# One projection for the context of all groups, and softmax division on the outputs, in the second attention of a two-layer trunk

## The chip, the cores and the metric

The kernel runs on one core of a Trainium2 chip. The metric is the time of one execution on the device, in microseconds (us). The five engines that the text names are TensorE (PE, with PEld for its weight loads), VectorE (DVE), ScalarE (ACT), GpSimd (POOL) and SyncE (SP), whose queue issues the DMA transfers. Each engine works through its own list of instructions in order and waits for the others by semaphores.

## The reference

A trunk of two layers over 1024 latent tokens and 256 context tokens, width 1024, 16 heads of 64. Layer 0 mixes by neighbourhood attention, layer 1 by sliding-window attention with grouped keys: four groups, each with four query heads, one key head and one value head. Every layer ends with a gated feed-forward network that has a convolution in it. In layer 1 the context has keys and values only, since its own stream ends there.

```
def attn_inputs(h, w_qkv, g_q, g_k, n_kv, with_q=True):
    ...
        kv = h @ w_qkv[:, D_MODEL:]
    k = rmsnorm(kv[..., :kv_w].reshape(bsz, t, n_kv, HEAD_DIM), g_k)
    v = kv[..., kv_w:].reshape(bsz, t, n_kv, HEAD_DIM)
...
def attend(q, k, v, bias=None, mask=None, sink=None):
    s = einsum(q, k) * HEAD_DIM ** -0.5      # and mask
    if sink is not None:
        s = concatenate([s, sink_col], axis=-1)
    p = softmax(s, axis=-1)[..., :-1]        # without the sink's column
    return einsum(p, v)
...
    # layer 1: queries see |i - j| <= 128 and all 256 context keys
    x = x + gt1 * (o @ w_out)
    h = modulate(rmsnorm(x, g_ffn[i]), sh2, sc2)
    x = x + gt2 * conv_ffn(h, ...)
```

All is float32. The kernel gets that accuracy from a fast product of rounded operands by splitting each operand into a rounded part (hi) and a remainder (lo) and adding three products: hi by hi, lo by hi, hi by lo.

## The kernel before

The kernel is a chain of stages: the first attention, the feed-forward of layer 0 (`ffn`, line 1246), the second attention (lines 2098 to 2350), the feed-forward of layer 1. Inside a stage the order of work is not written by hand. Each operation is given to a planner (`Sched`, line 61) with an engine (or a choice of two), a supposed duration, what it reads and writes, the ring buffers that it takes and gives back, and a rank (`key`). The planner plays a list schedule at build time, lower rank first among what is ready, and the instructions are issued in the order that comes out, one fixed order for each engine. So a change of a duration, a ring or a rank moves the whole stage, and an instruction that the chip finds late holds up everything behind it on its engine.

The rings that matter here are counted in `CAPS` (line 945): three raw buffers of 128x1024 for whatever a DMA brings in, four pairs of split weights (`w`, hi and lo), five probability rows `S`, two accumulators `mm`, two transposed blocks `pt`, two outputs `osb`. A ring gives out its buffers in turn, so the oldest has to be free before the next is taken.

The second attention has these kinds of operations.

- `plan_sw_qkv` (line 2118) makes queries, keys and values of one tile of 128 tokens for one group. Ten tiles belong to a group, in the order of `ORDER` (line 327): the two context tiles 8 and 9 first, then the latent tiles 0 to 7. A latent tile is 24 products of 384 columns (four query heads, a key head, a value head); a context tile is 24 products of 128 columns, since only key and value are wanted. Then come the norm over each head (a power on POOL, three small steps on DVE), rotation, the split into hi and lo, transposes on PE and copies to the key and query buffers. The ranks run from 16g, 1.6 for each tile.
- The weights of a group are four slabs (`Slabs`, line 405), each loaded into a raw buffer and split by ACT and POOL. The four slabs of group 0 are loaded and split in the feed-forward before (`plan_next`, line 2089, `AHEAD`), and stay in the four weight pairs over the stage's boundary.
- `plan_sw_su` (line 2245) with `plan_su` (line 504) is the attention of one block of 128 queries for one pair of heads, 16 of them in a group, ranks 16g + i + 7.5 (`LEAD1`). Scores against 256 context keys and up to 384 latent keys; on DVE the negated scores with mask and running minimum; on ACT the exponential with its sum (`exp`, line 563); on DVE the reciprocal of the sum (`rec`); on DVE or ACT the scaling of the 512 or 640 probabilities by it (`scale`, line 573). Then five transposes for each of the two heads, split, and products with the values, hi and lo packed side by side; the two halves are added into `osb`.
- For groups 0 to 2 the outputs go to memory (`o_dram`) and are fetched again at the end, since the buffers that hold the normed input are in use until the last QKV product. The last group's outputs stay on the chip.
- `plan_oproj1` (line 2315) is the output projection of the first 512 tokens: 8 blocks of 128 output columns, 24 products of 512 columns each, with rank 1000 (`OKEY`) and more, that is, after everything else. The fetched outputs are split into buffers that alias the normed input, so this may not start before the last QKV product of group 3 (`op1.gate`); the loads of outputs have the same gate, the loads of the projection's weights one a few tiles earlier (`w_gate`). The second 512 tokens are projected at the beginning of the feed-forward that follows.

Of the kernel before, what the change touches and what calls it, by code (L numbers as in the profile page):

```python
# [17 lines left out]
P = 128  # L18
# [208 lines left out]
def trunk_kernel(ctx, tc, xperm, xseq, cc, wmod, bmod, gnorm, na_wqkv, na_gq, na_gk, na_bias, na_wo,  # L227
                 sw_wqkv, sw_gq, sw_gk, sw_sink, sw_wo, rope_c, rope_s, band, w_up, conv, w_down, out):
# [15 lines left out]
    c_dram = dpool.tile([P, KT * TC], F32, name="c_dram")  # L244
    xa_dram = dpool.tile([P, KT * T], F32, name="xa_dram")
# [258 lines left out]
    def plan_su(sc, key, I, units, groups, psa, wk, reads, write, n_add):  # L504
# [28 lines left out]
        for k in range(2):  # L533
# [435 lines left out]
    AHEAD, NPRE = 4, 3  # L969
# [118 lines left out]
    def plan_na_su(n):  # L1088
# [71 lines left out]
        plan_su(sc, key, I, units, groups, psa, wk, reads, write, 1)  # L1160
# [859 lines left out]
    def plan_next(sc, KS, xn, bank, x_tile, plan_sums, plan_bc, plan_t, plan_hilo, u_done):  # L2020
# [68 lines left out]
        for i in range(AHEAD):  # L2089
            key = KS[5] - 4  # L2090
            sc.op("dma", 1.4, lambda e, i=i: slabs.load(i), reads=[("dw", 4, FT // 2 - 4, "r")], writes=[("slr", i)], key=key,
                  acq=[("raw", ("slr", i), 2)])
            sc.op("act", t_act(768), lambda e, i=i: slabs.hi(i), reads=[("slr", i), ("dw", 4, FT // 2 - 1, "wl", 0)],
                  writes=[("slh", i)], key=key, acq=[("w", ("slw", i), 1)], rel=[("slr", i)])
            sc.op("dve", 0.87, lambda e, i=i: slabs.lo(i, e), reads=[("slr", i), ("slh", i)],
                  writes=[("sll", i)], key=key, rel=[("slr", i)])

    slabs = Slabs(sw_wqkv, WL1)
    slabs.n_ahead = AHEAD
# [15 lines left out]
    op1 = Oproj(sc, 1, 0, 512, psa, [("q1", NKV - 1, tt, "acc") for tt in range(NT)], [],  # L2115
                [("q1", NKV - 1, WG1, "acc")])

    def plan_sw_qkv(n):
        g, tt = n // NT, ORDER[n % NT]
        key = n / NT * 16 + QKEY1  # L2120
        lat = tt < 8
# [3 lines left out]
        nh, c0 = (5, 0) if lat else (1, 256)  # L2125
        f = F1.setdefault(g, dict(q=[None] * 8, v=[None] * NT))
# [10 lines left out]
        def vhi(e):  # L2137
            vt = f["v"][tt] = fin.tile([P, P], F32R, tag="v" if lat else "vc", name="v", bufs=8 if lat else 4)
            copy(e, vt[:, 0:DH], J["raw"][:, 320:384])
        vuses = 2 * ((tt > 0) + 1 + (tt < 7)) if lat else 16  # L2140
        sc.op("act", t_act(64), vhi, reads=[K("raw")], writes=[K("vh")], key=key,
              acq=[("v" if lat else "vc", vk, vuses)], rel=[K("raw")])
# [7 lines left out]
        def qn(e):  # L2150
            J["qn"] = wk.tile([P, 5, DH], F32, tag="qn", name="qn", bufs=2)
            ENG[e].tensor_tensor(out=J["qn"][:, 5 - nh:], in0=J["raw"][:, c0:320].rearrange("p (h d) -> p h d", d=DH),
                                 in1=J["y"][:, :nh].unsqueeze(2).to_broadcast([P, nh, DH]), op=ALU.mult)
        sc.op("dve", t_dve(nh * DH), qn, reads=[K("raw"), K("y")], writes=[K("qn")], key=key,
              acq=[("qn", K("qn"), 2 if lat else 1)], rel=[K("raw")])
        spans = ((0, slice(0, 4), 4), (1, slice(4, 5), 1))
        if lat:
            def qa(e):
                J["a"] = wk.tile([P, 5, DH], F32, tag="qa", name="qa", bufs=2)
                for k, s, m in spans:  # L2160
                    ENG[e].tensor_tensor(out=J["a"][:, s], in0=J["qn"][:, s], in1=rc[:, tt, k:k + 1, :].to_broadcast([P, m, DH]),
                                         op=ALU.mult)
            sc.op(*QA, qa, reads=[K("qn")], writes=[K("a")], key=key, acq=[("qa", K("a"), 4)], rel=[K("qn")])

            def qb(e):
                J["b"] = wk.tile([P, 5, DH], F32, tag="qb", name="qb", bufs=2)
                for k, s, m in spans:
                    for d0, d1 in ((0, 32), (32, 0)):
                        ENG[e].tensor_tensor(out=J["b"][:, s, d0:d0 + 32], in0=J["qn"][:, s, d1:d1 + 32],
                                             in1=rs[:, tt, k:k + 1, d0:d0 + 32].to_broadcast([P, m, 32]), op=ALU.mult)  # L2170
            sc.op(*QB, qb, reads=[K("qn")], writes=[K("b")], key=key, acq=[("qb", K("b"), 1)], rel=[K("qn")])

            def qs(e):
                ENG[e].tensor_tensor(out=J["a"], in0=J["a"], in1=J["b"], op=ALU.add)
            sc.op("pool", t_pool(320), qs, reads=[K("b")], writes=[K("a")], key=key, rel=[K("b")])
        else:
            def qa(e):
                J["a"] = wk.tile([P, 5, DH], F32, tag="qa", name="qa", bufs=2)
                ENG[e].tensor_tensor(out=J["a"][:, 4], in0=J["qn"][:, 4], in1=gqk[:, 1, :], op=ALU.mult)
            sc.op(("pool", "dve"), (t_pool(64), t_dve(64)), qa, reads=[K("qn")], writes=[K("a")], key=key,  # L2180
                  acq=[("qa", K("a"), 2)], rel=[K("qn")])
# [13 lines left out]
        if lat:  # L2195
            def qhi(e):
                J["qhi"], J["qlo"] = [J["st"][:, 0:4, x * DH:(x + 1) * DH] for x in (0, 1)]
                act.activation(J["qhi"], J["a"][:, 0:4], AF.Copy)
            sc.op("act", t_act(256), qhi, reads=[K("a"), K("kd")], writes=[K("qh")], key=key, rel=[K("a")])

            def qlo(e):
                ENG[e].tensor_tensor(out=J["qlo"], in0=J["a"][:, 0:4], in1=J["qhi"].bitcast(F32), op=ALU.subtract)
            sc.op("pool", t_pool(256), qlo, reads=[K("a"), K("qh")], writes=[K("ql")], key=key,
                  rel=[K("a")])

        def trk(e):
# [4 lines left out]
              rel=[K("klt"), K("st")] + ([] if lat else [K("st")]))  # L2211
        kk, kl = (("kk", tt), ("kl", tt)) if lat else (("kkc", g), ("klc", g))
        first = [] if lat or tt == ORDER[0] else [kk, kl]

        def kev(e):
            if tt == ORDER[0]:
                f["kkc"] = fin.tile([P, TC], F32R, tag="kkc", name="kkc", bufs=2)
            dst = kkl1[:, tt * P:(tt + 1) * P] if lat else f["kkc"][:, (tt - 8) * P:(tt - 7) * P]
            copy(e, dst, J["pt2"][:, 0:P].bitcast(F32))
        sc.op("act", t_actp(128), kev, reads=[K("pt2")] + first, writes=[kk], key=key,  # L2220
              acq=[("kkc", kk, 32)] if tt == ORDER[0] else (), rel=[K("pt2")])

        def lev(e):
            if tt == ORDER[0]:
                f["klc"] = fin.tile([P, TC], F32R, tag="klc", name="klc", bufs=2)
            dst = kll1[:, tt * P:(tt + 1) * P] if lat else f["klc"][:, (tt - 8) * P:(tt - 7) * P]
            copy(e, dst, J["pt2"][:, P:2 * P].bitcast(F32))
        sc.op("act", t_actp(128), lev, reads=[K("pt2")] + first, writes=[kl], key=key,
              acq=[("klc", kl, 32)] if tt == ORDER[0] else (), rel=[K("pt2")])
        if lat:  # L2230
            def trq(e):
                J["pt"] = psa("pt", F32R)
                for i in range(4):
                    pe.transpose(J["pt"][:, i * P:(i + 1) * P], J["st"][:, i, :], idr)
            sc.op("pe", 0.43, trq, reads=[K("qh"), K("ql")], writes=[K("pt")], key=key, acq=[("pt", K("pt"), 1)],
                  rel=[K("st")])

            def qev(e):
                q = f["q"][tt] = fin.tile([P, 4, P], F32R, tag="q", name="q", bufs=8)
                copy(e, q.rearrange("p a b -> p (a b)"), J["pt"].bitcast(F32))  # L2240
            sc.op("act", t_actp(512), qev, reads=[K("pt")], writes=[qk], key=key, acq=[("q", qk, 8)], rel=[K("pt")])

    O = {}

    def plan_sw_su(n):
# [8 lines left out]
        for k in range(2):  # L2254
            hd = 2 * pr + k

            def get(hd=hd):
                q = f["q"][j]
                return dict(q=q[:, hd, :], kk=kkl1[:, ks], kl=kll1[:, ks], kkc=f["kkc"], klc=f["klc"],
                            mask=bandt[:, (lo - j + 1) * P:(hi - j + 2) * P], sink=sink[:, 4 * g + hd:4 * g + hd + 1])  # L2260
            units.append(dict(nl=(hi - lo + 1) * P, sink=1, get=get, mask_key=[], rel_c=[("q", g, j), ("kkc", g), ("klc", g)],
                              rel_l=[("q", g, j)]))
        reads = [("q", g, j), ("kkc", g), ("klc", g)]
        reads += [(x, t) for t in range(lo, hi + 1) for x in ("kk", "kl")]
        lst = [(8, 0), (9, P)] + [(b, TC + (b - lo) * P) for b in range(lo, hi + 1)]
        lst = [(lambda t=t: f["v"][t], ("v", g, t), [(0, c), (1, c)]) for t, c in lst]
        nj = 2 if g < NKV - 1 else 4
        ok = ("osb", g, j // nj, pr)
        heads = lambda t: t[0:DH].rearrange("p (h t) -> p h t", h=2)

        def write(sc, J, K):
            def add(e):
                if j % nj == 0:
                    f["o", pr] = O[j // 4, pr] = wk.tile([P, 512], F32, tag="osb", name="osb", bufs=2)
# [191 lines left out]
```

## Time and profile before

| what | value |
|---|---|
| median of 3 runs | 2849.25 us (2848.09 to 2849.77) |
| profiled execution | 2851.74 us |
| its span, first to last instruction | 2850.0 us |
| mean granted TensorE clock | 0.989 |
| PE busy over the span | 2784.4 us (98%) |
| DVE busy | 2324.1 us (82%) |
| ACT busy | 1713.2 us (60%) |
| POOL busy | 400.1 us (14%) |
| last product of the feed-forward before the stage | starts at 1677.55 us |
| first product of the next feed-forward stage | starts at 2145.18 us |

A row of windows gives a stretch in us from the start of the span, its length, then for each engine the busy time and in brackets the number of instructions, then the TensorE clock that was granted (1.00 is full), the share of the DMA engines in use, and GB/s. A row of the timeline gives start, duration, engine, line, operation, output and input tiles and, in square brackets, idle time before it and who ended it. A row of a group gives its form, how many there were, busy time and mean duration in ns, and idle time before them. All lines carry L51, a helper through which every instruction is recorded, so the tile names tell the operations apart: `mm` is an accumulator of QKV or of the projection, `h1chi` and `h1clo` the normed context, `S` the scores and probabilities, `sm` their sums, `slab` a raw weight slab, `oraw` a fetched output, `woraw` a raw block of projection weights. Matmuls are pipelined: a product's duration overlaps with that of the next, so dense products are counted by the distance of their starts.

### The profile page before, as it was taken

Reading aid. Unit: us, or ns where it says so; the run is one execution under the profiler, and the core shown is the slowest. Engines: PE = TensorE matmul, PEld = TensorE weight load, DVE = VectorE, ACT = ScalarE, POOL = GpSimd, SP = SyncE. Lnnn points to the kernel's source line nnn. Section 1 sums busy time; section 2 is a strip of 40 time slices with the busy share of each in tenths; the row PEclk is TensorE's granted clock in tenths of the full one; section 3 lists DMA queues with packets and bytes.
Section 4 is the critical chain, followed back from the end, with each engine's and each line's share of the span. In section 5 each row is a group of like instructions: output and inputs, shape, how many; then the busy total and the mean of one; then the engine's idle time right before and its main releaser. Section 6 shows DMA issues by size and latency. Waiting matters only on the chain.

```text
span 2850.0 us, 46124 instructions
## 1 busy us (share of the span) xinstructions
PE 2784.4 (98%) x16344; PEld 2455.3 (86%) x16344; DVE 2324.1 (82%) x5243; ACT 1713.2 (60%) x3382; POOL 400.1 (14%) x675
## 2 busy tenths in 40 slices
PE   6999999999999999999999999999999999999999
PEld 5999999998789987777788888999987788888887
DVE  7888888888688687877797787999987988888757
ACT  5877777778456554444454457888873554455443
POOL 1222212223000000000010006455520000000000
PEclk9999999999999999999999999999999999999999
DMA  6222222314745544444375551010234323324745
GB/s 247 65 95 80 83 67 75 96 60 125 250 142 192 183 162 140 154 142 160 135 258 194 181 169 29 13 34 16 73 128 138 116 105 111 111 93 149 253 148 182
DMA packets 140953, 367.20 MB, mean 129 GB/s; under 512 B 21425, under 2 KB 34225, under 8 KB 139313
## 3 DMA queue, kind: packets, MB, share of 16 engines
q1 hardware_dynamic: 140720, 364.25, 38.1%
q8 instruction: 129, 2.11, 0.3%
q14 instruction: 104, 0.84, 0.1%
HBM read 297.21 MB, written 66.98 MB: 128 GB/s over the span
## 4 chain that ended last, share of the span: by engine, by line
PE 69%; DVE 4%; ACT 2%; issue 1%; DMA 1%; DVEq 0%; ACTq 0%; SPq 0%
PE ua L51 17%; PE dn L51 15%; PE uc L51 13%; PE mm L51 6%; PE oacc L51 4%; PE ud L51 4%; PE pt L51 3%; PE pv L51 2%; PE dnc L51 2%; PE s L51 2%; DVE S L51 1%; PE mod L51 1%; ACT S L51 1%; DVE ptlo L51 1%; DVE x L51 0%
## 5 line engine op out<-in xcount | busy, mean ns | idle before, releaser
L51 ACT ACTIVATE whi<-wraw 128x512 fp32r<-128x512 f32 (+1 forms) x264 | 212.6, 806 | 203.6 <-PE uc L51 62.7
L51 DVE TENSOR_TENSOR wlo<-wraw,whi 128x512 fp32r<-128x512 f32 (+1 forms) x264 | 239.2, 907 | 45.3 <-ACT whi L51 44.8
L51 DVE TENSOR_TENSOR ptlo<-pt,pthi 128x512 fp32r<-128x512 f32 (+2 forms) x384 | 223.2, 595 | 48.6 <-ACT pthi L51 45.0
L51 PE MATMUL dn<-ghi,wlo 128*128 128x512 f32 x616 | 242.4, 394 | 0.0
L51 PE MATMUL dn<-ghi,whi 128*128 128x512 f32 x616 | 242.4, 394 | 0.0
L51 PE MATMUL dn<-glo,whi 128*128 128x512 f32 x616 | 242.3, 393 | 0.0
L51 ACT ACTIVATE pthi<-pt 128x512 fp32r<-128x512 f32 (+2 forms) x384 | 195.1, 524 | 71.1 <-PE pt L51 61.1
L51 ACT ACTIVATE S<-S,m 128x640 f32<-128x640 f32 (+3 forms) x288 | 220.8, 768 | 22.7 <-DVE m L51 19.6
L51 DVE SCALAR_TENSOR_TENSOR u<-c,cv,u 128x1023 f32<-128x1023 f32 x176 | 223.2, 1279 | 6.8 <-ACT u L51 5.8
L51 ACT ACTIVATE whi<-s 128x1024 fp32r<-128x1024 f32 (+1 forms) x120 | 113.3, 945 | 191.4 <-PE uc L51 137.4
L51 ACT ACTIVATE ghi<-graw 128x512 fp32r<-128x512 f32 x154 | 96.4, 631 | 190.2 <-PE dn L51 108.4
L51 PE MATMUL pt<-idr,S 128*128 128x128 f32 x1280 | 199.2, 278 | 6.8 <-DVE sm L51 2.6
L51 PE MATMUL mm<-whi,h0hi 128*128 128x384 f32 x512 | 181.1, 354 | 0.4 <-ACT qraw L51 0.4
L51 DVE TENSOR_TENSOR glo<-graw,ghi 128x512 fp32r<-128x512 f32 x154 | 105.4, 688 | 83.8 <-ACT ghi L51 76.4
L51 PE MATMUL mm<-wlo,h0hi 128*128 128x384 f32 x512 | 172.3, 337 | 0.0
L51 PEld LDWEIGHTS pt<-idr,S 128*128 128x128 f32 x1280 | 153.5, 143 | 17.4 <-DVE ptlo L51 3.9
L51 DVE TENSOR_TENSOR wlo<-s,whi 128x1024 fp32r<-128x1024 f32 (+1 forms) x120 | 129.6, 1080 | 40.6 <-ACT whi L51 40.5
L51 POOL TENSOR_TENSOR qy<-qv,mhalf 128x4 f32<-128x4 f32 (+2 forms) x120 | 126.2, 1052 | 227.0 <-DVE qv L51 197.0
L51 PE MATMUL pv<-ptlo,v 128*128 128x256 f32 (+1 forms) x688 | 153.9, 297 | 1.2 <-DVE ptlo L51 1.2
L51 PE MATMUL pv<-pthi,v 128*128 128x256 f32 (+1 forms) x688 | 147.7, 287 | 4.1 <-DVE osb L51 3.0
L51 PE MATMUL ua<-t12hi,whi 128*128 128x512 f32 x352 | 138.7, 394 | 5.5 <-ACT t12hi L51 3.9
L51 POOL TENSOR_TENSOR n1y<-n1v,mhalf 128x4 f32<-128x4 f32 (+1 forms) x9 | 9.2, 1025 | 953.3 <-DVE n1v L51 950.7
(315 smaller groups left out, 8906.4 us busy)
## 6 DMA issues: line engine op xcount, KB each, us to landing
wraw<-in_w_up_dram SPq DMA_DIRECT2D x132, 512.0 KB, 3.4
wm<-in_wmod_dram SPq DMA_DIRECT2D x80, 512.0 KB, 4.0
wraw<-in_w_down_dram SPq DMA_DIRECT2D x44, 512.0 KB, 3.5
graw<-g_dram SPq DMA_DIRECT2D x44, 512.0 KB, 4.4
wraw<-in_w_down_dram SPq DMA_DIRECT2D x88, 256.0 KB, 3.0
graw<-g_dram SPq DMA_DIRECT2D x66, 256.0 KB, 2.8
slab<-in_na_wqkv_dram SPq DMA_DIRECT2D x32, 384.0 KB, 3.7
woraw<-in_na_wo_dram SPq DMA_DIRECT2D x24, 512.0 KB, 4.4
```

The lines of the kernel that those rows point to most:

```text
L51: r = f(*a, **k)
```

## The change

Context keys and values are no longer made group by group. One step, `plan_ctx_kv`, projects both context tiles onto the 512 columns of all groups' keys and values (48 products of 512 columns), norms, splits and transposes them, and keeps them for the whole stage. The feed-forward before brings these weights (`sw_ckv`, four pieces of 128x1024) over the boundary instead of the four slabs of group 0, which are now loaded and split within the stage. The QKV step has eight tiles in a group, with ranks 2 apart.

The reciprocal and the scaling of the probabilities go. The sum of each exponential row is written to a column of a table (`RS`), and the unscaled probabilities are transposed and multiplied with the values. For each group (for the last one, each half) one reciprocal of the table, a transpose, a copy and a store put the reciprocals into memory (`r_dram`). They are fetched again, each row repeated over 64 partitions, beside the stored outputs, and the outputs are multiplied by them before they are split.

At the end of the plan the stored outputs of the first 512 tokens get ranks from 57 on instead of 994 on, the first two of them with the earlier gate `w_gate`, the first four weight blocks of the projection ranks from 60.5 instead of 1000. The second half of x for the residual goes to the buffer of the context keys and so waits for the last score products. The last outputs of group 3 use the ring `st`.

```
@@ plan_su
-               scale=-1.0, accum_out=J["sm"][:, k, 0:1])
+               scale=-1.0, accum_out=sums(k) if sums else J["sm"][:, k, 0:1])
             sc.op("act", t_act(n) + 0.187, exp, reads=parts, writes=[K("P", k)], key=key)
+            if sums:
+                continue
@@ plan_next
-        for i in range(AHEAD):
-            key = KS[5] - 4
-            sc.op("dma", 1.4, lambda e, i=i: slabs.load(i), ...)
+        for i in range(4):
+            key = KS[5] - 30
...
+            sc.op("dma", 1.8, load, ..., key=KS[5] - 4, acq=[("raw", ("slr", i), 2)])
+            sc.op("act", t_act(1024), hi, ..., key=key, acq=[("w", ("slw", i), 1)], rel=[("slr", i)])
+            sc.op("dve", t_dve(1024) + 0.03, lo, ..., key=key, rel=[("slr", i)])
@@
+    def plan_ctx_kv():
+        hh, hl = h[2]
+        for i in range(4):
+            def mm(e, i=i):
+                for tt in range(2):
...
+                    for k in (2 * i, 2 * i + 1):
+                        wh, wl = [a[:, k % 2 * 512:k % 2 * 512 + 512] for a in CW[i]]
+                        for m, (a, w) in enumerate(((hh, wh), (hl, wh), (hh, wl))):
+                            pe.matmul(acc[tt], a[:, k, sl], w, start=(k == 0 and m == 0), stop=(k == KT - 1 and m == 2))
+            sc.op("pe", 12 * t_pe(512), mm, writes=[("ckv", "acc")], key=-300, ...)
...
+            CK["k"] = hpool.tile([P, 8, 256], F32R, tag="hclo", name="ckc", bufs=1)
...
+                CK["v", tt] = fin.tile([P, NKV, P], F32R, tag="vc", name="vc", bufs=2)
@@ plan_sw_qkv
-        g, tt = n // NT, ORDER[n % NT]
-        key = n / NT * 16 + QKEY1
+        g, tt = divmod(n, 8)
+        key = n * 2 + QKEY1
@@
+    def plan_recip(g, js, key):
+        a, n = 4 * js[0], 4 * len(js)
+        def rec(e):
+            dve.reciprocal(RS[g][:, a:a + n], RS[g][:, a:a + n])
...
+            pe.transpose(RS["pt", g, a][:n, :P], RS[g][:, a:a + n], idf)
...
+            RS["sb", g, a] = fin.tile([32, P], F32, tag="rst", name="rst", bufs=2)
+            act.activation(RS["sb", g, a][:n], RS["pt", g, a][:n, :P], AF.Copy)
...
+        sc.op("dma", 0.6, lambda e: dma.dma_start(r_dram[g, a:a + n], RS["sb", g, a][:n]), ...)
+
+    def r_rows(kt, c, k):
+        a = 16 * c + 4 * (2 * (kt % 2) + k)
+        return r_dram[kt // 2, a:a + 4, :].rearrange("j q -> (j q)").unsqueeze(0).to_broadcast([DH, 512])
@@ plan_sw_su
+        ring = "osb" if g < NKV - 1 or j < 4 else "st"
...
+        if g < NKV - 1:
+            if i == 15:
+                plan_recip(g, list(range(8)), 16 * g + 17 + LEAD1)
+        elif i in (7, 15):
+            c = j // 4
+            plan_recip(g, list(range(4 * c, 4 * c + 4)), key)
...
+            sc.op("dma", 1.8, load, reads=[("rs", g, c)], writes=[rk], key=key, acq=[("raw", rk, 2)])
+            for p in range(2):
...
+                op1.split(c, (c, 2 * g + p), 512, ...)
@@ the plan of the stage
+    for i in range(4):
+        sc.hold("w", ("cw", i), 1)
+    plan_ctx_kv()
...
+        slabs.engs = WL1 if g else WL0
         for j in range(4):
-            if 4 * g + j >= slabs.n_ahead:
-                slabs.plan(sc, 4 * g + j, 16 * g + QKEY1 if g else -200, NT)
-        for k in range(NT):
-            plan_sw_qkv(NT * g + k)
+            slabs.plan(sc, 4 * g + j, 16 * g + QKEY1 if g else -200, 8)
+        for k in range(8):
+            plan_sw_qkv(8 * g + k)
@@ plan_oproj1
                     dma.dma_start(R[c, kt][:, :512], o_dram[1][kt, :, 512 * c:512 * c + 512])
+                    for k in range(2):
+                        dma.dma_start(R[c, kt][k * DH:(k + 1) * DH, 512:], r_rows(kt, c, k))
-                key = OKEY + 6 * (c - 1) + kt
-                sc.op("dma", 1.0, load, reads=[("od", kt, c)] + op1.gate, writes=[r], key=key, ...)
+                key = OKEY + kt if c else 57 + 0.5 * kt
+                gate = op1.gate if c or kt > 1 else op1.w_gate
+                sc.op("dma", 1.8, load, reads=[("od", kt, c), ("rs", kt // 2, c)] + gate, writes=[r], key=key - 0.5, ...)
+                sc.op(("pool", "dve"), ..., R[c, kt][:, :512] * R[c, kt][:, 512:] ..., key=key)
-            op1.weights(dt, sw_wo[dt % KT], OKEY + dt, KT, ...)
+            op1.weights(dt, sw_wo[dt % KT], 60.5 + dt if dt < 4 else OKEY + dt, KT, ...)
```

More of the change, by code (lines that the diff above doesn't have):

```diff
@@ L2230, in plan_sw_qkv @@
[L2230 to L2241, printed above, removed]
@@ L2273, in add @@
                 if j % nj == 0:
-                    f["o", pr] = O[j // 4, pr] = wk.tile([P, 512], F32, tag="osb", name="osb", bufs=2)
+                    f["o", pr] = O[j // 4, pr] = wk.tile([P, 512], F32, tag=ring, name="osb", bufs=2)
                 if g < NKV - 1:
@@ L2320, in load @@
                 dma.dma_start(xt[k].rearrange("p k t -> p (k t)"), x_dram[:, 2048 * k:2048 * (k + 1)])
-            sc.op("dma", 3.2, load, reads=op1.gate, writes=[("xc", k)], key=OKEY + k)
+            sc.op("dma", 3.2, load, reads=op1.gate + [("su1", NKV - 1, j, pr, "sc") for j in range(8) for pr in range(2)] * k,
+                  writes=[("xc", k)], key=OKEY + k)
         def evac(dt, I):
```

272 lines of the change are left out of this document (191 added, 81 removed).

## The prediction

> **What bounds the kernel now.** I looked at the page first, for the shares over the whole span, then at windows over the second attention (the only stretch the change touches), then at the timeline of TensorE (PE) and of the DMA queue at its two ends, last at the groups by form.
>
> ```profile
> span 2850.0 us, 46124 instructions
> ```
> ```profile
> core 0: us, PE busy (x) PEld busy (x) DVE busy (x) ACT busy (x) POOL busy (x), PEclk, DMA share, GB/s
> 1742.00:2057.00 315.00, 310.15 (x2295) 301.95 (x2294) 295.87 (x1048) 276.66 (x695) 168.79 (x349) 0.99 0.10 28
> 2057.00:2077.00 20.00, 16.22 (x83) 12.97 (x83) 18.82 (x62) 14.94 (x34) 14.40 (x21) 0.74 0.53 185
> 2077.00:2145.00 68.00, 68.00 (x396) 59.66 (x395) 54.86 (x141) 46.07 (x93) 12.19 (x21) 1.00 0.45 148
> 1678.00:1742.00 64.00, 58.84 (x336) 57.32 (x337) 46.69 (x141) 35.70 (x87) 25.39 (x46) 0.87 0.21 72
> ```
>
> The stage runs from 1678 to 2145. In its long middle (first row) PE is busy 310.15 of 315 us at clock 0.99, while VectorE (DVE) has 295.87 and ScalarE (ACT) 276.66. DVE is close, but PE is the full one. Only the two ends have holes: 64 us with 58.84 busy at clock 0.87, and 20 us with 16.22 busy at 0.74. So two things are worth time here: products that disappear, and holes at the ends. Relief of DVE or ACT in the middle is not.
>
> Busy times overlap from one product to the next, so the price of a product is its distance to the next one in a dense run. Three pairs of timeline rows give it: 384 columns, 128 columns (context rows of a middle group), 512 columns (the last feed-forward products).
>
> ```profile
> 1698.16 0.33 PE L51 MATMUL mm<-whi,h1hi 128*128 128x384 f32 x1
> ...
> 1698.68 0.33 PE L51 MATMUL mm<-whi,h1hi 128*128 128x384 f32 x1
> ```
> ```profile
> 1871.65 0.27 PE L51 MATMUL mm<-whi,h1chi 128*128 128x128 f32 x1
> ...
> 1872.32 0.28 PE L51 MATMUL mm<-whi,h1chi 128*128 128x128 f32 x1
> ```
> ```profile
> 1675.69 0.39 PE L51 MATMUL dn<-ghi,whi 128*128 128x512 f32 x1
> ...
> 1677.55 0.40 PE L51 MATMUL dn<-ghi,wlo 128*128 128x512 f32 x1
> ```
>
> Three steps in 0.52 us: 0.173 at 384 columns. Six in 0.67: 0.112 at 128. Eight in 1.86: 0.23 at 512. Four times the columns cost only twice the time; that is the core of the first part of the change.
>
> The holes, in windows cut where the granted clock changes (same columns):
>
> ```profile
> 1677.50:1680.90 3.40, 2.11 (x15) 1.56 (x15) 3.40 (x5) 2.31 (x4) 0.00 (x0) 1.00 1.01 383
> 1680.90:1684.30 3.40, 3.40 (x18) 3.39 (x17) 3.16 (x6) 1.43 (x4) 0.00 (x0) 0.50 0.96 289
> ...
> 1687.70:1691.10 3.40, 3.40 (x13) 3.40 (x13) 1.92 (x11) 0.94 (x4) 1.16 (x2) 0.50 0.77 298
> ...
> 1708.20:1711.60 3.40, 1.29 (x8) 0.97 (x7) 2.90 (x10) 1.37 (x4) 1.79 (x3) 1.00 0.00 0
> 1711.60:1715.00 3.40, 3.40 (x13) 3.40 (x12) 2.24 (x11) 1.18 (x4) 3.30 (x7) 0.50 0.02 5
> ...
> 1749.10:1752.60 3.50, 1.56 (x13) 1.27 (x11) 3.43 (x13) 3.45 (x8) 1.78 (x3) 1.00 0.35 112
> 1752.60:1756.00 3.40, 3.40 (x17) 3.21 (x17) 3.36 (x12) 2.57 (x10) 2.51 (x3) 0.50 0.17 41
> ...
> 2063.20:2066.60 3.40, 2.19 (x10) 1.43 (x11) 3.40 (x14) 1.94 (x5) 3.40 (x8) 1.00 0.84 311
> 2066.60:2070.00 3.40, 2.48 (x8) 1.33 (x7) 3.21 (x14) 3.40 (x10) 2.65 (x2) 0.50 0.14 48
> ```
>
> A window in which PE stood for 1.2 to 2.1 us is followed by one at clock 0.50, so a hole costs itself and up to 1.7 us more. After the hole at 1677.5 the clock stays at 0.50 for three windows (1680.9 to 1691.1).
>
> **The change part by part.**
>
> *Context products.* Before, each of four groups runs 48 products of 128 columns (8 slices, 3 terms, 2 context tiles); after, 48 products of 512 columns run once. In groups 1 to 3 the products vanish from the full PE: 3 x 48 x 0.112 = **-16.1 us**. Group 0 belongs to the start.
>
> *The start.* Two more edits meet here: the four weight pairs held over from the feed-forward now carry the context columns, so the slabs of group 0 have to be fetched and split inside this stage; and the second half of the norm runs beside it.
>
> ```profile
> 1710.83 0.45 PE L51 MATMUL mm<-whi,h1hi 128*128 128x384 f32 x1 [2.11 <-ACT qraw L51]
> ```
> ```profile
> 1682.79 67.45 SPq L51 DMA_DIRECT2D slab<-in_sw_wqkv_dram  x6
> ```
> ```profile
> slab<-in_sw_wqkv_dram SPq DMA_DIRECT2D x10, 384.0 KB, 3.5
> ```
> ```profile
> L51 ACT ACTIVATE whi<-slab 128x768 fp32r<-128x768 f32 x5 | 4.2, 843 | 2.0 <-PE dn L51 1.8 <-DMA slab<-in_sw_wqkv_dram 0.2
> ...
> L51 DVE TENSOR_TENSOR wlo<-slab,whi 128x768 fp32r<-128x768 f32 x4 | 3.6, 954 | 0.3 <-ACT whi L51 0.3
> ```
>
> Before, 33 us lie between the last feed-forward product (ends near 1677.8) and tile 4 (1710.83, after a wait of 2.11 for the norm). After: context products 48 x 0.23 = 11.0, to 1688.8. The queue is free for slabs at 1682.79 as before, behind the writing and reloading of x; the DMA engines are full (share 0.96, then 0.77 of 3.4 us) to about 1690.3. The wider splits ahead of the x evictions on DVE (0.954 x 1024/768 = 1.27 each, an estimate) move this by about one split: slab 0 lands near 1691.5, plus 0.84, 0.95 and two hand-overs: PE starts tile 0 near 1693.6, a hole of 4. Slabs 2 and 3 wait for a raw buffer (the norm's sums, then slab 0) and come 3.5 + 0.84 + 0.95 later, near 1699; until then the first halves of tiles 0 and 1 keep PE busy. Then four tiles of 24 x 0.173 = 16.6, one window at half clock as after the holes at 1708 and 1749 (1.7), and 24 small products (broadcast of the norm, transposes of the context keys) at 0.112 = 2.7: tile 4 near 1715, 4 later than before. But the norm started 3 us earlier and should be done, so no wait stands ahead of tile 4, and the half window behind it, at 1711.6, is gone (1.7): **+2 us**. Ends: -4 if the slabs land under the context products (no hole, no half window), +9 if slabs 2 and 3 are also waited for, one landing of 3.5 each. I take the middle because the queue's order is the same as before. The two accumulators wait for ACT to copy them before tiles 0 and 1 can start; the hole covers that, and without it it would cost two copies.
>
> Here a rule bears. The Trainium skill, "TensorE: Matmul & The Clock Gate", section "What's actually happening", lets the clock fall after at least one idle window of about 3.4 us and rise after one busy window. This trace disagrees on both: 1.3 us of standing sufficed at 1677.5, and three windows stayed at 0.50 with PE busy 3.40 of 3.40. By the rule my hole of 4 us costs one half window, the 1.7 I took; by the row at 1680.9 it may cost three, and the sum would be 3.4 us higher.
>
> *The division.* Per unit a reciprocal and a scaling of the probabilities go (128 of each).
>
> ```profile
> L51 DVE TENSOR_SCALAR S<-S,sm 128x640 f32<-128x640 f32 x60 | 36.0, 600 | 0.5
> ...
> L51 DVE RECIPROCAL sm<-sm 128x1 f32<-128x1 f32 x122 | 18.6, 155 | 4.4 <-ACT S L51 3.3
> ```
> ```profile
> L51 ACT ACTIVATE S<-S,sm 128x640 f32<-128x640 f32 x34 | 28.1, 829 | 4.6 <-DVE sm L51 4.4
> ```
> ```profile
> L51 DVE TENSOR_TENSOR ptlo<-pt,pthi 128x512 fp32r<-128x512 f32 x126 | 84.6, 683 | 4.6 <-ACT pthi L51 3.5
> ```
>
> That frees 36.0 + 18.6 us of DVE and 28.1 of ACT in these rows alone. In the middle it buys nothing, PE being full. It shortens the way from exponential to transpose, which counts where PE waits: the hole at 1749.1 (1.94 us, and 1.7 at half clock) lies under busy ACT and DVE; the one near 1728 I leave. I take **-3**, ends 0 and -7 (both holes). Added: five transposes of row sums of 128 columns at 0.112, **+0.6** on PE; five evictions, five stores of the sums, 32 broadcast loads, 16 multiplies of 128x512 at about 0.68 (the last row's size on DVE). Stores of groups 0 to 2 stand on the queue ahead of next-group slabs; those are asked for seven ranks early, so 0, and a landing of 3.5 if that cover goes. The wider splits at the end of the feed-forward lie under PE products: 0 beyond the shift counted above.
>
> *The end.* QKV products end near 2057; then PE has only attention until the output projection can begin, at 2076.53.
>
> ```profile
> 2076.53 0.61 PE L51 MATMUL mm<-o0hi,whi 128*128 128x512 f32 x1
> ```
> ```profile
> 2145.18 0.39 PE L51 MATMUL oacc<-o1hi,whi 128*128 128x512 f32 x1
> ```
> ```profile
> 2058.68 2.76 SPq L51 DMA_DIRECT2D oraw<-o_dram  x2
> ...
> 2068.59 26.48 SPq L51 DMA_DIRECT2D oraw<-o_dram  x9
> 2095.98 0.33 SPq L51 DMA_DIRECT2D woraw<-in_sw_wo_dram  x1
> 2102.62 0.32 SPq L51 DMA_DIRECT2D oraw<-o_dram  x1
> 2108.25 0.33 SPq L51 DMA_DIRECT2D woraw<-in_sw_wo_dram  x1
> ```
>
> The hole is 3.8 us in 20, plus about 4 us lost at half clock (a mean of 0.74 is 10.4 us at half; 8 us of them busy): 7.9. With DVE busy 18.82 of 20, it is DVE that feeds too slowly; without scalings, and with the first two stored tiles fetched and multiplied ahead of the gate, projection products come earlier. Against it: those two tiles sit in the ring of three raw buffers until the gate, so one W_o column block is prepared ahead instead of four. I take half: **-4**, ends -7.9 and the ring case below. The second half of x is now loaded into the buffer of the context keys, after the last score product; the first four column blocks (4 x 24 x 0.23 = 22 us) cover it; uncovered, PE would stop at two full accumulators.
>
> **Sum:** -16.1 + 2 - 3 + 0.6 - 4 = -20.5. The profiled execution took 2851.74 (span 2850.0), 2.5 above the median 2849.25; 2831.2 for it, **2828.7** for the median. I take the feed-forwards as unchanged.
>
> **The rivals.**
>
> *Slabs starve the start.* +9 instead of +2 and none of the 3: -16.1 + 9 + 0.6 - 4 = -10.5, **2839**. For it: full DMA engines to 1690.3. Against: half tiles fill the time.
>
> *All holes close.* -16.1 - 4 - 7 + 0.6 - 7.9 = -34.4, **2815**. For it: each hole after 1728 lies under DVE or ACT. A gain of 50 and more (DVE's relief in full) is excluded by PE's 310 of 315.
>
> *Slower: the raw ring sets the end.* Between 2058.68 and 2108.25 thirteen loads pass the ring: 3.8 us each, 11.4 in a buffer. After, 10 stored tiles, 10 blocks of W_o and 2 tiles of reciprocals still have to pass it behind the gate: 22 x 3.8 = 84 us, just under today's 88 (2057 to 2145). It decides from 4.75 us a load ((88 + 16.5)/22, 16.5 being the other gains). A second landing (3.5) and a multiply (0.7) in each buffer make 5.2: 114 us, +26 at the end, in all +9.5: **2859**. For it: the order of the ring is fixed. Against: six tiles are for the second half and need not be in by the end, and 3.8 is a pace that nobody pressed.
>
> *Gains and losses cancel* (slabs starve, ring near 4.75): within 6 us of **2849**.
>
> **How the numbers follow.** Forecast 0.57 (its own range 2819 to 2837); slabs 0.12; holes close 0.16; ring 0.10; cancel 0.05. About 0.2% is what a measurement of this kernel can tell from no change. Faster by more: 0.57 + 0.12 + 0.16 = 0.85; within: 0.05; slower: 0.10. The range 2812 to 2844 holds the first three but for thin edges.
>
> **What would show it.** No 128-column context products after the start, and 48 of 512 columns in one run of about 11 us from 1678; a hole of some 4 us before the first 384-column product; the second-half tiles without a wait; no scaling group on DVE or ACT, and the middle shorter by about 16 us with PE still full. At the end the first projection product within 10 us of the last QKV product. Wrong if PE in the middle shows new holes (then DVE or ACT order sets it), if the start loses more than 9, or if PE waits at the end for stored tiles or W_o.

## The result

The changed kernel takes 2832.02 us (median of 4 runs, 2831.11 to 2833.21) against 2849.51 us (2848.09 to 2850.26) on the same chip: a ratio of 0.9933, 95% interval 0.992 to 0.9946, or 17.5 us less. The forecast was 20.5 us less. The profiled execution has a span of 2830.6 us.

Windows of the changed kernel, columns as in the prediction: the long middle, the end, then the start.

```profile
core 0: us, PE busy (x) PEld busy (x) DVE busy (x) ACT busy (x) POOL busy (x), PEclk, DMA share, GB/s
1742.00:2038.80 296.80, 294.88 (x2181) 289.94 (x2180) 260.26 (x867) 251.40 (x638) 155.41 (x328) 1.00 0.12 34
2038.80:2042.60 3.80, 3.80 (x30) 3.67 (x29) 3.75 (x13) 3.77 (x10) 3.00 (x8) 1.00 0.11 41
2042.60:2104.00 61.40, 56.42 (x356) 47.66 (x356) 57.17 (x147) 47.38 (x103) 25.41 (x39) 1.00 0.54 181
...
1677.60:1681.40 3.80, 0.38 (x2) 0.01 (x1) 3.80 (x6) 3.06 (x4) 0.00 (x0) 0.81 0.97 311
1681.40:1688.00 6.60, 6.58 (x18) 5.23 (x19) 6.08 (x9) 2.99 (x5) 0.00 (x0) 0.59 0.94 327
1688.00:1696.00 8.00, 8.00 (x41) 6.76 (x40) 2.88 (x5) 3.15 (x6) 0.00 (x0) 1.00 0.87 315
1696.00:1715.00 19.00, 19.00 (x120) 18.59 (x119) 18.13 (x40) 13.34 (x27) 5.06 (x5) 1.00 0.22 62
1715.00:1720.60 5.60, 0.69 (x3) 0.43 (x2) 3.59 (x14) 0.94 (x3) 3.17 (x4) 0.73 0.00 0
```

The middle is shorter, its clock is 1.00 instead of 0.99, and DVE is busy for 260.26 of 296.80 us (88%, before 94%). At the end PE is full up to the projection, but then stands for 5 of 61.4 us, where it was full before. The start has two holes, the windows with 0.38 and 0.69 us of PE. The first is new; the second, ahead of tile 4, was 2.11 us long before. Here is the first one on PE's timeline, and DVE's timeline beside it.

```profile
1677.59 0.39 PE L51 MATMUL dn<-ghi,wlo 128*128 128x512 f32 x1
1681.42 0.77 PE L51 MATMUL mm<-whi,h1chi 128*128 128x512 f32 x1 [3.44 <-ACT sq L51]
1681.99 0.63 PE L51 MATMUL mm<-whi,h1clo 128*128 128x512 f32 x1
```
```profile
1673.83 0.75 DVE L51 SCALAR_TENSOR_TENSOR xn<-dn,modc,xn 128x512 f32<-128x512 f32 x1 [2.19 <-PE dn L51]
1674.49 2.35 DVE L51 TENSOR_TENSOR wlo<-ckv,whi 128x1024 fp32r<-128x1024 f32 x2
1676.76 2.06 DVE L51 SCALAR_TENSOR_TENSOR xn<-dn,modc,xn 128x512 f32<-128x512 f32 x3
1678.74 1.22 DVE L51 TENSOR_TENSOR wlo<-ckv,whi 128x1024 fp32r<-128x1024 f32 x1
1679.87 1.40 DVE L51 SCALAR_TENSOR_TENSOR xn<-dn,modc,xn 128x512 f32<-128x512 f32 x2
```

The row names ACT, whose `sq` ends at 1681.28, but the product has no use for that. At 1681.27 ends the sixth eviction `xn<-dn` of the feed-forward's eight accumulators (an eviction is the step that empties an accumulator), and the first context product needs a bank that it frees; in e4 and e6 below, this wait names `xn`. Three splits of context weights (`wlo<-ckv`, 1.2 us each, rank KS[5]-30) stand between the evictions. The second hole is ahead of tile 4.

```profile
1714.93 0.34 PE L51 MATMUL mm<-wlo,h1hi 128*128 128x384 f32 x1
1720.17 0.69 PE L51 MATMUL mm<-whi,h1hi 128*128 128x384 f32 x1 [4.91 <-ACT qraw L51]
1720.65 0.52 PE L51 MATMUL mm<-whi,n1lo 128*128 128x384 f32 x1
```

PE waits for a copy of an accumulator into `qraw`, whose two buffers are held by tiles 0 and 1: their small DVE steps stand behind the norm, the context chain and two slab splits, and DVE is full from 1696 to 1715 (18.13 of 19.00). The end, on PE's timeline: the last QKV product and the first one of the projection.

```profile
2038.85 0.35 PE L51 MATMUL mm<-wlo,h1hi 128*128 128x384 f32 x1
...
2042.61 0.39 PE L51 MATMUL mm<-o0hi,whi 128*128 128x512 f32 x1
```

The table gives stretches of the stage in us for the kernels of this study: start (last feed-forward product to first score product), middle (to the last QKV product), end (to the first product of the next feed-forward). "Lost" (waits, half clock and all else) is the stretch less its products at the distance that they have in dense runs (0.110, 0.119, 0.176, 0.228 us for 128, 256, 384, 512 columns). Two profiles of one kernel differ by 1 to 2 us in a stage, mostly in its two ends.

| kernel | start | middle | end | stage | lost in start / middle / end |
|---|---|---|---|---|---|
| before | 48.1 | 331.8 | 87.8 | 467.6 | 10.8 / 11.7 / 9.9 |
| changed | 53.7 | 307.6 | 87.4 | 448.7 | 13.6 / 0.9 / 8.7 |
| e1 context alone | 52.6 | 306.2 | 98.1 | 457.0 | 12.5 / 6.6 / 12.9 |
| e2 division alone | 45.0 | 323.3 | 90.2 | 458.6 | 7.8 / 2.6 / 12.4 |
| e3 both, old ranks | 54.0 | 307.2 | 94.0 | 455.2 | 13.9 / 0.7 / 15.0 |
| e4 splits behind | 55.2 | 307.6 | 87.4 | 450.1 | 15.1 / 0.9 / 8.6 |
| e5 chain later | 50.4 | 306.3 | 87.2 | 443.9 | 9.8 / 0.3 / 8.1 |
| e6 and splits on POOL | 51.3 | 306.3 | 87.6 | 445.2 | 10.7 / 0.3 / 8.5 |
| e7 no multiplies | 52.8 | 307.1 | 84.6 | 444.4 | 12.7 / 0.6 / 5.5 |
| e8 and slabs first | 47.8 | 306.3 | 88.0 | 442.1 | 7.2 / 0.3 / 8.9 |

### The profile page after: what moved, and what is told of

Read it like the earlier page. It is cut to its first block, busy times and chain, and to the rows that moved or that the text cites. A ratio compares the mean times of both kernels' runs of the same rounds, so it can differ in the third digit from the quotient of the medians.

```text
span 2830.6 us, 45660 instructions
## 1 busy us (share of the span) xinstructions
PE 2763.8 (98%) x16205; PEld 2431.7 (86%) x16205; DVE 2291.1 (81%) x5012; ACT 1687.7 (60%) x3313; POOL 387.9 (14%) x652
## 5 line engine op out<-in xcount | busy, mean ns | idle before, releaser
L51 ACT ACTIVATE S<-S,m 128x640 f32<-128x640 f32 (+3 forms) x288 | 220.6, 767 | 23.0 <-DVE m L51 18.8
L51 PEld LDWEIGHTS pt<-idr,S 128*128 128x128 f32 x1280 | 150.9, 141 | 16.6 <-DVE ptlo L51 5.1
L51 POOL TENSOR_TENSOR qy<-qv,mhalf 128x4 f32<-128x4 f32 (+1 forms) x112 | 119.6, 1068 | 154.5 <-DVE qv L51 136.7
L51 PEld LDWEIGHTS dn<-ghi,wlo 128*128 128x128 f32 x616 | 115.5, 187 | 28.4
L51 PEld LDWEIGHTS dn<-glo,whi 128*128 128x128 f32 x616 | 115.5, 188 | 27.5
```

The costliest lines, as they stand in the source:

```text
L51: r = f(*a, **k)
```

## The experiments

### The three parts by themselves (e1, e2, e3)

The change undone to its first part (against the changed kernel), built up from before with its second part, and all of it without the new ranks:

```
e1, against the changed kernel (and the ranks as in e3)
-        plan_su(sc, key, I, units, ..., write, sums)
+        plan_su(sc, key, I, units, ..., write)
-        (plan_recip, the loads of r_rows, all multiplies by them, the ring "st")
e2, against the kernel before
+        plan_su(..., write, sums), plan_recip, r_rows, the multiplies; ring "st" for the last outputs
e3, against the changed kernel
-                key = OKEY + kt if c else 57 + 0.5 * kt
-                gate = op1.gate if c or kt > 1 else op1.w_gate
+                key = OKEY + 6 * (c - 1) + kt
+                gate = op1.gate
-            op1.weights(dt, ..., 60.5 + dt if dt < 4 else OKEY + dt, ...)
+            op1.weights(dt, ..., OKEY + dt, ...)
```

> Context keys and values at once, nothing else: the division stays on the probabilities and the ranks at the end are those of before. My theory (context products -16.1, start +5.6 as measured, both holes behind the first scores are the division's doing and stay here): 2849.5 - 16.1 + 5.6 = 2839, with the windows near 1728 and 1749 (shifted by the start) still followed by half clock. Rival (the holes closed because the context tiles no longer pass through the tile loop, not because of the division): 2839 - 7 = 2832, the same as with all three parts.

> The division on the outputs, nothing else: context products per group as before, ranks at the end as before. My theory: -7 from the two holes behind the first scores, +0.6 for the five transposes, the long middle unchanged within 1 us because PE is full there, the end between 0 and -4: 2843 (2838 to 2844). Rival (the relief of DVE and ACT is worth nothing, the holes have another cause): 2850. Rival (the relief counts all along the middle): under 2835.

> All of the change but the ranks at its end, which are those of before (stored tiles at OKEY + 6*(c-1) + kt behind the gate, W_o blocks at OKEY + dt). Forecast as on record (the ranks and early fetches bring -4): 2836, and the gap of some 19 us between the last QKV product and the first projection product is back, with its holes and half clock. Rival (the end is bound by how much work DVE has there, the ranks only move the waits): within 1 us of 2832.

Measured, with 2851.37 us for before on that chip: e1 2840.64 us, ratio 0.9959 (0.9946 to 0.9971). e2 2841.32 us, 0.9961 (0.9949 to 0.9974). e3 2838.96 us, 0.9949 (0.9935 to 0.9963). Windows of the middle, in this order:

```profile
1742.00:2035.00 293.00, 289.31 (x2105) 280.13 (x2103) 280.01 (x985) 262.62 (x644) 165.01 (x331) 1.00 0.12 33
```
```profile
1742.00:2043.00 301.00, 299.06 (x2247) 294.70 (x2246) 257.55 (x864) 248.06 (x644) 154.94 (x329) 1.00 0.10 29
```
```profile
1742.00:2040.00 298.00, 296.28 (x2192) 291.06 (x2191) 260.51 (x868) 253.34 (x641) 159.32 (x336) 1.00 0.11 29
```

The first two times are near what I expected (2839, 2843), but the table shows other reasons. In the middle each part alone removes much of the 11.7 us that was lost: the context part 5.1, the division 9.1, both 11.0. Each alone ends the two half-clock windows behind the first scores (clock 1.00 in all three rows, and from the first score product to 1742 as well), so neither my theory (the division alone does it) nor its rival (the context tiles alone) holds. What the parts gain in the middle is partly the same time, so their stages, 10.6 and 9.0 us shorter, do not add up: together 12.4. With the context part alone DVE is busy 280.01 of 293 us (96%), 6.6 us are still lost, and 13 attention steps remain after the last QKV product instead of 11. That is most of why its end is the longest: 7.3 us more of products than before, and 3.0 more lost. Of the start of e2, 3 us shorter, I make no gain of the division: there the half clock after the last feed-forward product held for one window, before for three.

The ranks are worth 6 to 8 us by the profiles: 455.2 against 448.7 us of stage (446.9 in a second profile of the changed kernel), nearly all of it at the end, where e3 loses 15.0 us against 8.7. By the ratios, 0.9949 and 0.9933, they are worth nearer 5. With the old ranks the projection starts 22 us after the last QKV product.

```profile
2040.80:2062.80 22.00, 16.90 (x119) 14.59 (x117) 21.17 (x62) 18.63 (x45) 12.97 (x19) 0.97 0.44 145
2062.80:2104.10 41.30, 36.80 (x233) 31.49 (x232) 33.13 (x90) 28.38 (x61) 16.40 (x23) 0.98 0.50 153
```

So the end gets longer by both other parts (94.0 against 87.8) and shorter by the ranks, and comes out level.

### The first hole of the start (e4)

```
         for i in range(4):
-            key = KS[5] - 30
+            key = KS[5] - 4
```

> All of the change, but the splits of the context weights have the rank of before (KS[5]-4), so that the evictions of the feed-forward's accumulators go ahead of them on DVE. My theory (the hole at 1677.6 to 1681.4 is the wait for those evictions): first context product near 1678.1 instead of 1681.4, no half clock behind it, 3 to 6.5 us gained: 2826 to 2829. Rival A (DVE is full from there to 1720 and sets tile 4 and the first scores, so the gain is lost in the second hole): 2831 to 2833. Rival B (the slabs are now late and PE stands ahead of tile 0, as the prediction had it): a hole of 3 to 5 us near 1689, 2830 or more.

Measured on the same chip: 2833.02 us, ratio 0.9932 (0.992 to 0.9945): no gain. PE's waits from 1677 to 1734 (us in total, times, the longest):

```profile
PE mm L51 <- ACT qraw L51: 4.2, 1, 4.2
PE mm L51 <- ACT S L51: 4.1, 1, 4.1
PE mm L51 <- DVE xn L51: 1.2, 1, 1.2
```

The wait for the evictions shrinks from 3.4 to 1.2 us, now named as such, and no half clock follows it. But PE now stands 4.1 us ahead of tile 0: later splits keep the raw buffers longer, so the slabs are asked for behind the reload of x, at 1685.7 instead of 1680.0. That is rival B. Rival A is not excluded by this run, since the second hole is still there with 4.2 us. The hole that the prediction had ahead of tile 0 is real; in the changed kernel the early splits avoid it and pay with the other hole.

### The second hole, and both (e5, e6, e8, e9)

```
e5, against the changed kernel (all steps of the chain behind the first copy)
-            sc.op(..., key=-250, ...)    # or -240
+            sc.op(..., key=5.0, ...)
e6, against e5
-                dve.tensor_tensor(out=CW[i][1], in0=CW[i, "r"], ...)
+                pool.tensor_tensor(out=CW[i][1], in0=CW[i, "r"], ...)
e8, against e6
-    for j in range(0, KT, 2):
-        dma.dma_start(xs[1].tiles[j // 2], x_dram[...])
+    for j in range(0, KT, 2):
+        sc.op("dma", 1.8, lambda e, j=j: dma.dma_start(xs[1].tiles[j // 2], x_dram[...]),
+              writes=[("x1", j), ("x1", j + 1)], key=-205)
```

> All of the change, but the steps that turn the raw context keys and values into transposed, split ones have rank 5.0 in the plan instead of -250 and -240: they come behind the norm of the second half and the first tiles' steps, and still ahead of the first scores (7.5). My theory (the second hole, 1714.9 to 1720.2, is there because DVE is full from 1696 to 1715 with the norm, this chain and two slab splits, and the first tiles' small steps stand behind them): about 4 us less of DVE ahead of tile 4, the hole shrinks from 4.9 us to 1 or less and its two half windows go: 2825 to 2828, ratio 0.991 to 0.992. Rival (the hole is set by the slow powers on POOL and the hand-overs behind the norm, whatever stands on DVE): hole within 1 us of 4.9, ratio 0.993. Rival (the chain then stands in the way of the first scores): the hole moves behind 1725, ratio 0.993.

> As the run with the later chain, and the four splits of the context weights go to POOL, which has nothing to do between 1677 and 1690. My theory (DVE sets the start: evictions, splits and sums stand in one line): first context product near 1678, no hole and no half clock behind it; a smaller hole remains ahead of tile 0 if the slabs land late. 3 to 6 us less than the run with the later chain alone. Rival (the transfers set the start, as they did when the splits were moved behind the evictions: the 1.2 us and 4.1 us stood where 3.4 us had been): a hole of 3 to 5 us ahead of the first 384-column product and a time within 1 us of the run with the later chain alone.

Measured, with 2850.77 us for before: e5 2826.93 us, ratio 0.9921 (0.9907 to 0.9935); e6 2828.8 us, 0.9927 (0.9913 to 0.994). PE's waits from 1674 to 1734 in e5:

```profile
PE mm L51 <- ACT sq L51: 3.4, 1, 3.4
PE pt L51 <- ACT st L51: 2.4, 1, 2.4
PE mm L51 <- ACT qraw L51: 0.6, 2, 0.4
```

The wait for `qraw` falls from 4.9 to 0.6 us: it was set by the order on DVE. Half of it comes back as a wait of the chain's own transposes (`pt <- st`), which stand in PE's fixed order; 3 to 5 us of stage remain as gain. In e6 the first hole is gone as well (first context product 0.6 us after the last feed-forward product), and the whole of it returns ahead of tile 0. The SP queue, ACT and PE there:

```profile
1678.98 3.84 SPq L51 DMA_DIRECT2D x<-x_dram  x4
1682.87 17.11 SPq L51 DMA_DIRECT2D slab<-in_sw_wqkv_dram  x7
```
```profile
1691.25 0.84 ACT L51 ACTIVATE whi<-slab 128x768 fp32r<-128x768 f32 x1 [5.06 <-DMA slab<-in_sw_wqkv_dram]
```
```profile
1693.65 0.69 PE L51 MATMUL mm<-whi,h1hi 128*128 128x384 f32 x1 [5.21 <-ACT S L51]
```

This is the start as the prediction had worked it out: slabs asked for at 1682.87, the first landing near 1691.2, PE at 1693.6. The rival of this run holds. What is left is the place of the slabs in the queue, behind 2 MB of x.

> As the run with the later chain and the context splits on POOL, and the reload of the second half of x is put into the plan behind the loads of the first two slabs; only the order of the DMA queue differs from that run. My theory (what is left of the start is the landing of slab 0 behind 2 MB of reload: issued at 1682.9, landed near 1691.2, PE at 1693.6 after 5.2 us of waiting): slab 0 issued near 1679 to 1680, landed by 1686, first 384-column product within 1 us of the last context product, no half clock there; 4 to 7 us less than that run: 2822 to 2825, ratio 0.990 to 0.9915. Rival (the slabs' own splits on ACT and DVE, or slabs 2 and 3, hold tiles 0 and 1 instead): PE still stands 2 us or more before 1700 and the gain is under 3 us. Rival (the reload is now late and the norm with it): a wait ahead of tile 4 grows by what is gained.

> The changed kernel as it is, beside the run with the slabs first on the same chip, to set the two side by side: 2832, ratio 0.993.

Measured side by side, with 2849.11 us for before: e8 2825.36 us (2824.24 to 2826.07), ratio 0.9913 (0.9899 to 0.9926); the changed kernel 2832.27 us (2830.24 to 2833.0), 0.9935 (0.9922 to 0.9949). Two windows of e8, up to the wait for the chain's transposes and that wait:

```profile
1678.00:1708.40 30.40, 29.81 (x161) 27.24 (x160) 26.09 (x44) 19.35 (x35) 9.32 (x7) 1.00 0.62 224
1708.40:1712.00 3.60, 0.59 (x5) 0.27 (x3) 3.18 (x15) 0.63 (x1) 2.30 (x2) 0.88 0.00 0
```

PE is full at full clock through context products and tiles 0 to 3; one hole of 3 us is left. My theory holds for place and order; the time fell by 3.4 us against e6, where I expected 4 to 7. This kernel is faster than the kernel before and the changed one. Against e5, which only moves ranks, its lead (0.9913 to 0.9921) is too small for these runs to tell.

### The end (e7, e10, e11)

```
e7, against the changed kernel
-                sc.op(("pool", "dve"), ..., out=R[c, kt][:, :512], in0=R[c, kt][:, :512], in1=R[c, kt][:, 512:], op=ALU.mult)
e10, against e8
-                key = OKEY + kt if c else 57 + 0.5 * kt
+                key = OKEY + 5 + kt if c else 57 + 0.5 * kt
```

> All of the change, but the twelve multiplies of the stored tiles by their reciprocals are left out (their rows are still loaded), so the outputs of groups 0 to 2 stay undivided. My theory (the end is set by DVE and POOL, which the multiplies load with 12 steps of 0.68 to 1.29 us): the end from the last QKV product to the next stage's first product shrinks by 3 to 6 us from 87.4: 2826 to 2829, ratio 0.9915 to 0.9925. Rival (the multiplies lie beside other work, the waits come from the order of PE's own queue): within 1 us, ratio 0.993.

> As the run with the slabs first, and the six stored tiles of the second half (their loads, multiplies and splits) have ranks 5 higher (OKEY + 5 + kt), so that half of them come after the last score step. My theory (PE's 8 to 9 us of waits between the first projection product and the last attention product come from DVE and POOL, which carry the multiplies and splits of both halves there): 1 to 4 us less from the last QKV product to the next stage's first product, which took 88.0 in that run (2031.9 to 2119.9): 2821 to 2824. Rival (the buffers of the raw ring then come free too late for the W_o blocks, or the next stage waits for its second half): PE waits after 2097, and the time is the same or up to 4 us longer: 2825 to 2829.

> The run with the slabs first, again, to set the run with the second half later beside it on one chip: 2825, ratio 0.991.

Measured on the chip of e5: e7, which leaves the multiplies out, takes 2828.19 us, ratio 0.9924 (0.9911 to 0.9936). Its end:

```profile
2041.80:2100.50 58.70, 56.61 (x362) 48.35 (x360) 54.71 (x147) 47.45 (x103) 16.10 (x32) 1.00 0.60 189
```

PE stands for 2.1 us where it stood for 5.0, and the end is 2.8 us shorter than in the changed kernel (2.1 against its second profile). So the twelve multiplies cost 2 to 3 us, at or under the lower edge of what I expected (3 to 6); the times alone, 0.9924 and 0.9933, would not tell it. PE's waits at the end of the changed kernel, 2039 to 2104, all name DVE; these are the two largest:

```profile
PE pt L51 <- DVE ptlo L51: 2.5, 4, 1.5
PE pv L51 <- DVE osb L51: 1.3, 2, 0.8
```

In e7 the first has shrunk to 0.2 us and the second is gone. e10 took 2824.08 us, 0.991 (0.9895 to 0.9925), beside e8 again with 2825.57 us, 0.9913 (0.9896 to 0.9929). Its end (86.2 us) lies between the two profiles of e8 (88.0 and 85.9): the rank of the second half decides nothing that these runs can tell. About 5 us are still lost at the end of e7, 2.1 of them with PE standing; where the rest goes stays open.

## Why the prediction was right, and where it was not

The total was right and the range held it, but two steps were wrong by about 7 us each, with opposite signs. That they cancelled was luck. The prediction counted the start up to tile 4 and the rest from there:

| step of the sum | forecast | measured | from |
|---|---|---|---|
| context products and five transposes | -16.1 + 0.6 | -16.6 | products from tile 4 on, at dense paces |
| start, up to tile 4 | +2 | +9.3 | 42.6 us from the last feed-forward product, before 33.3 |
| division (holes in the middle) | -3 | -10.3 | time lost from tile 4 to the last QKV product, 13.0 to 2.7 |
| end | -4 | -1.2 | time lost behind the last QKV product |
| sum | -20.5 | -18.8 | stage 467.6 to 448.7 |

- *Context products.* Right: they left a PE that was full. The sum overlooked twelve transposes of context keys that leave groups 1 to 3 with them (1.3 us).
- *The start.* Wrong in size and in place. The failing step is "The wider splits ahead of the x evictions on DVE (...) move this by about one split": the splits held the accumulators that the context products need, which the prediction took as free. And "the norm started 3 us earlier and should be done, so no wait stands ahead of tile 4" looked only at the norm, not at what else DVE had to do beside it. The norm's first step on DVE (`n1v`) came 3 us later, at 1695.94 after 1692.83. The wait of 2.11 us, which the prediction took for one for the norm, was already one for `qraw` before: that copy waited for a small step of a tile (`qn`), while the norm's last split had ended at 1709.57.

```profile
1709.68 0.49 DVE L51 TENSOR_TENSOR qn<-qraw,qy 128x320 f32<-128x320 f32 x1
1710.29 0.49 ACT L51 ACTIVATE qraw<-mm 128x384 f32<-128x384 f32 x1 [1.83 <-DVE qn L51]
```

In the changed kernel the same wait grew. +9.3 is just over the limit that the prediction itself named (9). That "the queue's order is the same as before" failed too: the first two slabs went out among the stores and reloads of x, the first ahead of the whole reload.

```profile
1679.98 0.33 SPq L51 DMA_DIRECT2D slab<-in_sw_wqkv_dram  x1
...
1684.13 0.48 SPq L51 DMA_DIRECT2D slab<-in_sw_wqkv_dram  x1
1687.81 1.27 SPq L51 DMA_DIRECT2D x<-x_dram  x3
```

Their splits began at 1688.08, under the context products, and PE began tile 0 at 1695.77 without a wait. The forecast's order and its landing near 1691 came true only in e6 (1691.25, PE at 1693.65). The rival "slabs starve the start" gave the right size by a mechanism that did not act here.
- *Half clock.* The first hole was followed by 6.60 us at a mean clock of 0.59. The Trainium skill, "TensorE: Matmul & The Clock Gate", section "What's actually happening", gives a free-running window of about 3.4 us; by it a hole can fall among the windows in another place in each run. The traces agree: the same hole of 3.4 us cost two half-clock windows in the changed kernel, one in its second profile and one in e5. The prediction counted one such window in the start; the changed kernel has four there, two behind each hole (before: three and one).
- *The division.* "In the middle it buys nothing, PE being full" with -3 for the holes is the step that failed. Of the 11.7 us lost in the middle 8.9 lay between the first score product and 1757: two half-clock windows (1.7 each), the holes before them, and small waits. 4.0 of these lay ahead of 1742, outside the row with PE's 310.15 of 315 us. Only 0.5 is left there in the changed kernel. Past 1757 the middle lost 2.8 us, so there PE was nearly as full as the prediction said. Nor is the gain the division's alone: by itself it took 9.1 of the 11.7, the context part by itself 5.1. The rival "all holes close" had this right for the middle.
- *The end.* That "projection products come earlier" was right: 3.8 us after the last QKV product instead of 19.1, with no half clock. But the time that filled this gap was taken from later, where PE now waits. The ranks gave 5 to 8 us (forecast for the whole end: 4); the multiplies, which the prediction listed without a price at the end, took 2 to 3 back; and DVE is as busy there as it was (75.79 of 87.43 us, before 73.42 of 87.78).
- *The ring rival.* It did not act. In the changed kernel's queue 15 loads passed the raw ring between these two rows, 3.35 us each, below the 4.75 at which it would decide:

```profile
2042.41 0.33 SPq L51 DMA_DIRECT2D oraw<-o_dram  x1
...
2092.63 8.17 SPq L51 DMA_DIRECT2D woraw<-in_sw_wo_dram  x4
```

## What to carry to other kernels

When work moves over a stage boundary, go through every buffer that the first instruction of the new stage takes (accumulator banks, too), and find who frees it and what stands ahead of that on its engine. A hole that one removes at a boundary tends to come back at the next ring (e4, e6); here only the kernel that put the evictions, the loads in the queue and the engine's order right together (e8) was rid of both, down to one wait of 3 us, though moving ranks alone (e5) had most of the gain. And a "full" engine in a long window can still lose some per cent: set its products at their dense pace against the window's length, piece by piece, before saying that relief of the other engines buys nothing. Here most of the loss stood in the first 30 us.

## What I had not expected of the hardware

How long PE must stand for the clock to fall is not told by the share of a window alone. Before, a window with PE busy 2.11 of 3.40 us was followed by one at 0.50. In e1, at the end, PE was busy for less, and the next window was at full clock:

```profile
2052.90:2056.40 3.50, 1.79 (x11) 1.24 (x12) 3.31 (x12) 2.91 (x6) 0.00 (x0) 1.00 0.24 75
2056.40:2059.80 3.40, 2.94 (x19) 2.35 (x20) 3.25 (x11) 3.29 (x9) 1.25 (x3) 1.00 0.24 77
```

Here the standing is spread over several short waits, there 1.1 of 1.3 us were one piece. But that is not the reason either: in the trace of before, PE stood for one piece of 1.29 us from 834.73, the busy time of the window was 2.11 us again, and the clock stayed full.

```profile
834.40:837.80 3.40, 2.11 (x18) 1.91 (x17) 3.40 (x6) 2.94 (x6) 0.00 (x0) 1.00 0.25 55
837.80:841.20 3.40, 3.40 (x31) 3.40 (x30) 3.40 (x6) 1.63 (x3) 0.00 (x0) 1.00 0.66 236
```

What decides in such windows stays open. Nor is it plain how long the clock stays down: behind the last feed-forward product it was at 0.50 for three windows before (1680.9 to 1691.1) and for one in e2, with the same 128-column products following, and for one or two in those kernels with the context part that have a hole there, where 512-column products follow.
